# Clearing the semaphores during the last store, with SyncE waiting for that store in GpSimd's place

## Chip, cores and metric

One core of one Trainium2 chip. The metric is the device time of one execution in microseconds (us); the kernel before has a median of 121.06 us over three runs (121.06 to 121.23). Engines are called PE (TensorE), DVE (VectorE), ACT (ScalarE), POOL (GpSimd) and SP (SyncE), as in the profile.

## The reference

```python
x, y: (1024, 4096) float32
z = x + y
out = 0.5 * z * (1 + np.tanh(np.sqrt(2 / np.pi) * (z + 0.044715 * z ** 3)))
```

An addition followed by the tanh form of GELU, elementwise: 33.55 MB are read and 16.78 MB are written.

## The kernel before

Each input is seen as 128 partitions of 32,768 numbers. SP's queue issues four loads of 8,192 columns of x and four of y in turn (`load_x`, `load_y`), then three stores of 16,384, 10,240 and 6,144 columns (`store`, L130 to L132). The arithmetic runs in sixteen chunks of 2,048 columns: POOL adds y into the z tile (DVE does it for chunk 0; L145), ACT squares into PSUM (L150), DVE forms the polynomial (L156), ACT applies the sigmoid (L161) and DVE multiplies back into z (L168). The order on each engine is written out by hand in four lists, one for each queue (SP, POOL, ACT, DVE), and issued from these in the `while any(queues)` loop (L209). None of this is touched by the change.

After the last list is empty, `tc.close()` (lines shown as L223 in the profile) adds the end of the program. It is a block of instructions of its own, behind the block with the work: SP waits for every DMA and for the other engines, two barriers over all five engines follow, and POOL clears the eleven semaphores 99 to 109, which the program counted with, so that the next execution starts from zero. A barrier here is: SP, ACT, PE and DVE each add one to semaphore 96 with a DRAIN, POOL waits until that is four, takes it back, adds four to semaphore 97, and each of the others waits for that and takes one off.

`wait_late` (L26 to L58), called last in the kernel (L225), edits that end block. SP's wait for everything loses the wait for the last store, whose semaphore is 103 (it has to count 32: two DMAs with 16 each). POOL's pair, a DRAIN and an EVENT_SEMAPHORE_RANGE_CLEAR of 99 to 109, moves from between the two barriers to behind the second one, and the DRAIN gets the wait for semaphore 103. So the last instructions of the program are, in the kernel before:

```
SP    waits for all DMAs but the last store, for DVE and POOL
all   barrier 1
all   barrier 2
POOL  DRAIN, waits for semaphore 103 >= 32
POOL  EVENT_SEMAPHORE_RANGE_CLEAR 99 to 109
```

`begin_early` (L11 to L23) moves the first two loads ahead of the barrier at the start; the change doesn't touch it.

Of the kernel before, what the change touches and what calls it, by code (L numbers as in the profile page):

```python
# [25 lines left out]
def wait_late(nc):  # L26


    body, end = nc.main_func.blocks[1:3]
    SP, POOL = mybir.EngineType.SP, mybir.EngineType.Pool  # L30
    last = [i for i in body.instructions if isinstance(i, mybir.InstDMACopy)][-1]
    (sem,) = [u.id for u in last.sync_info.on_update]
    all_done = end.instructions[0]
    clear = next(i for i in end.instructions if isinstance(i, mybir.InstDrain) and i.is_reset_sema)
    assert all_done.engine == SP and clear.engine == POOL and clear.sync_info is None
    waits = all_done.sync_info.on_wait
    its = [w for w in waits if w.id == sem]
    assert len(its) == 1
    rest = [w for w in waits if w.id != sem]

    def drain(old, waits, **reset):
        return mybir.InstDrain(
            name=old.name, engine=old.engine, debug=old.debug,
            sync_info=mybir.SyncInfo(on_wait=waits, on_update=[]), **reset
        )

    at = end.instructions.index(clear)
    clears = [
        drain(
            clear, its, is_reset_sema=True,  # L50
            reset_range_start=clear.reset_range_start, reset_range_stop=clear.reset_range_stop,
        ),
        end.instructions[at + 1],
    ]
    assert isinstance(clears[1], mybir.InstISA) and clears[1].engine == POOL
    del end.instructions[at : at + 2]
    end.instructions[0] = drain(all_done, rest, is_reset_sema=False)
    end.instructions.extend(clears)  # L58


@with_exitstack
def kernel(
# [160 lines left out]
    tc.compile()  # L223
    begin_early(nc, 2)
    wait_late(nc)  # L225


# [28 lines left out]
```

## Time and profile before

| what | value |
|---|---|
| median of three runs | 121.06 us (121.06 to 121.23) |
| the profiled execution, its own time | 121.08 us |
| its span, first to last instruction of the program | 118.9 us (118.914 in the trace) |
| outside the span, of the time | 2.17 us |
| DVE busy | 73.7 us, 62% |
| POOL busy | 69.7 us, 59% |
| ACT busy | 61.0 us, 51% |
| DMA queue | 98.6% of 16 engines' span, 50.33 MB |
| last store (3,072 KB), issue to landing | 11.9 us |

Times in the profile count from the span's start. An instruction that belongs to an engine's sequencer (waits, barriers, DRAIN, the clearing of semaphores, DMA issues) is shown with a q behind the engine's name and isn't counted as busy. A view of one source line lists, for each engine and operation, how many there were, their shortest, median and longest time in ns, and the first and last start in us. The table of stretches gives for each stretch its length, each engine's busy time, and the share of the DMA engines' time that was used. The trace also holds the moment of every change of a semaphore, that of the runtime's semaphores too, after the span's end.

### The profile page before, as it was taken

Reading aid. Unit: us, or ns where it says so; the run is one execution under the profiler, and the core shown is the slowest. Engines: PE = TensorE matmul, PEld = TensorE weight load, DVE = VectorE, ACT = ScalarE, POOL = GpSimd, SP = SyncE. Lnnn points to the kernel's source line nnn. Section 1 sums busy time; section 2 is a strip of 40 time slices with the busy share of each in tenths; the row PEclk is TensorE's granted clock in tenths of the full one; section 3 lists DMA queues with packets and bytes.
Section 4 is the critical chain, followed back from the end, with each engine's and each line's share of the span. In section 5 each row is a group of like instructions: output and inputs, shape, how many; then the busy total and the mean of one; then the engine's idle time right before and its main releaser. Section 6 shows DMA issues by size and latency. Waiting matters only on the chain.

```text
span 118.9 us, 170 instructions
## 1 busy us (share of the span) xinstructions
DVE 73.7 (62%) x35; ACT 61.0 (51%) x34; POOL 69.7 (59%) x19
## 2 busy tenths in 40 slices
DVE  0000000635799995749999958999994999990000
ACT  4000000064888865197698657888829769800000
POOL 0000000699995199999959999959999990000000
DMA  7989898989999898989899998998898889999996
GB/s 254 452 364 518 353 529 353 518 364 474 408 430 452 364 518 353 529 353 518 364 474 408 408 474 353 529 529 353 353 683 375 353 353 441 441 441 441 397 397 265
DMA packets 1584, 50.33 MB, mean 423 GB/s; under 512 B 176, under 2 KB 176, under 8 KB 176
## 3 DMA queue, kind: packets, MB, share of 16 engines
q1 hardware_dynamic: 1584, 50.33, 98.6%
HBM read 33.55 MB, written 16.78 MB: 423 GB/s over the span
## 4 chain that ended last, share of the span: by engine, by line
DMA 51%; POOL 26%; POOLq 4%; DVE 4%; DVEq 2%; ACT 2%; issue 0%; SPq 0%
DMA y<-in_y_dram 51%; POOL z L145 26%; POOLq L223 4%; DVE w L156 2%; DVEq L223 2%; DVE z L168 2%; ACT w L150 2%; SPq L121 0%; POOLq L145 0%
## 5 line engine op out<-in xcount | busy, mean ns | idle before, releaser
L145 POOL TENSOR_TENSOR z<-z,y 128x2048 f32<-128x2048 f32 x15 | 69.4, 4661 | 28.2 <-DMA y<-in_y_dram 28.2
L150 ACT ACTIVATE w<-z 128x2048 f32<-128x2048 f32 x16 | 30.1, 1882 | 37.6 <-DVE z L145 21.4
L156 DVE SCALAR_TENSOR_TENSOR w<-w,z 128x2048 f32<-128x2048 f32 x16 | 36.7, 2295 | 11.2 <-ACT w L150 11.0
L168 DVE TENSOR_TENSOR z<-w,z 128x2048 f32<-128x2048 f32 (+1 forms) x17 | 35.9, 2155 | 0.0
L161 ACT ACTIVATE w<-w 128x2048 f32<-128x2048 f32 x16 | 29.7, 1855 | 4.4 <-DVE w L156 4.3
L145 DVE TENSOR_TENSOR z<-z,y 128x2048 f32<-128x2048 f32 x1 | 2.3, 2292 | 20.4 <-DMA y<-in_y_dram 20.4
L208 ACT ACT_TABLE_LOAD x1 | 1.3, 1283 | 1.3 <-PEq L240 1.3
L207 DVE MEMSET one<- 128x1 f32 x1 | 0.1, 59 | 1.3 <-PEq L240 1.3
L240 POOL MEMSET const-float32-0.0<- 128x1 f32 x1 | 0.1, 99 | 0.2 <-issue 0.2
L208 ACT ACTIVATE one<-one 128x1 f32<-128x1 f32 x1 | 0.2, 203 | 0.0
L240 POOL MEMSET const-bfloat16-1.0<- 128x1 bf16 x1 | 0.1, 101 | 0.0
L240 POOL MEMSET const-uint8-127<- 128x1 uint8 x1 | 0.1, 101 | 0.0
L240 POOL MEMSET const-float32-1.0<- 128x1 f32 x1 | 0.1, 98 | 0.0
## 6 DMA issues: line engine op xcount, KB each, us to landing
z<-in_x_dram SPq DMA_DIRECT2D x4, 4096.0 KB, 31.3
y<-in_y_dram SPq DMA_DIRECT2D x4, 4096.0 KB, 22.2
out_dram<-z SPq DMA_DIRECT2D x1, 5120.0 KB, 15.8
out_dram<-z SPq DMA_DIRECT2D x1, 3072.0 KB, 11.9
out_dram<-z SPq DMA_DIRECT2D x1, 22.0
```

Source lines behind the costliest of these rows:

```text
L145: eng.tensor_add(out=zt[:, a:b], in0=zt[:, a:b], in1=yt[s][:, o : o + b - a])
L150: nc.scalar.activation(out=wt[c], in_=zt[:, a:b], func=act.Square, scale=root)
L156: nc.vector.scalar_tensor_tensor(out=wt[c], in0=wt[c], scalar=c1, in1=zt[:, a:b], op0=alu.add, op1=alu.mult)
L161: nc.scalar.activation(out=wt[c], in_=wt[c], func=act.Sigmoid)
L168: ins = nc.vector.tensor_mul(out=zt[:, a + o : a + o + n], in0=wt[c][:, o : o + n], in1=zt[:, a + o : a + o + n],)
L207: nc.vector.memset(one, 0.0)
L208: nc.scalar.activation(out=one, in_=one, func=act.Sigmoid)
L223: tc.compile()
L240: nc = _bacc.Bacc("TRN2", target_bir_lowering=False, num_devices=1)
```

## The change

Only `wait_late` changes. POOL's DRAIN and its clearing stay where `tc.close()` put them, between barrier 1 and barrier 2, and no longer wait for anything. The one clearing of 99 to 109 becomes two, 99 to 102 and 104 to 109, which leave out semaphore 103. At the very end SP gets one new instruction, an EVENT_SEMAPHORE that waits until 103 has counted 32 and takes 32 off. The end of the program becomes:

```
SP    waits for all DMAs but the last store, for DVE and POOL
all   barrier 1
POOL  DRAIN
POOL  EVENT_SEMAPHORE_RANGE_CLEAR 99 to 102
POOL  EVENT_SEMAPHORE_RANGE_CLEAR 104 to 109
all   barrier 2
SP    EVENT_SEMAPHORE, waits for semaphore 103 >= 32, subtracts 32
```

```diff
-    at = end.instructions.index(clear)
-    clears = [
-        drain(
-            clear, its, is_reset_sema=True,
-            reset_range_start=clear.reset_range_start, reset_range_stop=clear.reset_range_stop,
-        ),
-        end.instructions[at + 1],
-    ]
...
-    del end.instructions[at : at + 2]
-    end.instructions[0] = drain(all_done, rest, is_reset_sema=False)
-    end.instructions.extend(clears)
...
+    parts = []
+    for f, e in ((first, sem), (sem + 1, stop)):
+        if f < e:
+            nc.gpsimd.sem_clear(range(f, e))
+            parts.append(nc.cur_bb.bb.instructions.pop())
+    end[at + 1 : at + 2] = parts
+    end.append(
+        mybir.InstEventSemaphore(
+            name=clear.name, engine=mybir.EngineType.SP, debug=clear.debug,
+            sync_info=mybir.SyncInfo(
+                on_wait=[its],
+                on_update=[
+                    mybir.SyncUpdate(
+                        sync_type="semaphore", id=sem, ant_name=its.ant_name,
+                        update_mode="sem-sub-imm", update_value=its.wait_value,
+                    )
+                ],
+            ),
         )
+    )
```

SP's first wait of the end block keeps the same set of waits as before. The instructions of PE, ACT and DVE are the same, and so are all of POOL's and SP's up to the end block.

## Prediction

> **What bounds the kernel now.** I read the page first, then the table of stretches for the end, then the view of the line of the closing code (L223), then SP's waits.
>
> ```profile
> span 118.9 us, 170 instructions
> ...
> q1 hardware_dynamic: 1584, 50.33, 98.6%
> ...
> DMA y<-in_y_dram 51%; POOL z L145 26%; POOLq L223 4%; DVE w L156 2%; DVEq L223 2%; DVE z L168 2%; ACT w L150 2%; SPq L121 0%; POOLq L145 0%
> ...
> out_dram<-z SPq DMA_DIRECT2D x1, 3072.0 KB, 11.9
> ```
>
> The one DMA queue is full for 98.6% of the span: the kernel is bound by its 50.33 MB. The chain of waits names the loads and POOL's adds, but it stops at 106.7 us, where the last multiply (L168) releases the last store; the 12.2 us behind that are the store and the end of the program. They are read from stretches:
>
> ```profile
> core 0: us, DVE busy (x) ACT busy (x) POOL busy (x), PEclk, DMA share, GB/s
> ...
> 107.00:112.50 5.50, 0.00 (x0) 0.00 (x0) 0.00 (x0) 1.00 0.91 390
> 112.50:118.26 5.76, 0.00 (x0) 0.00 (x0) 0.00 (x0) 1.00 0.93 401
> 118.26:118.70 0.44, 0.00 (x0) 0.00 (x0) 0.00 (x0) 1.00 0.00 0
> 118.70:118.92 0.22, 0.00 (x0) 0.00 (x0) 0.00 (x0) 1.00 0.00 0
> ```
>
> No engine computes after 107; data moves until 118.26. Then 0.44 us pass in which nothing moves and the store's last counts arrive on semaphore 103 (the trace has the sixteenth at 118.689), and 0.22 us that are POOL's alone:
>
> ```profile
> L223 POOLq EVENT_SEMAPHORE  x2: 17/17/17, 112.0 to 112.1; - x2
> L223 SPq EVENT_SEMAPHORE  x1: 17/17/17, 112.2 to 112.2; - x1
> L223 ACTq EVENT_SEMAPHORE  x1: 17/17/17, 112.2 to 112.2; - x1
> L223 DVEq EVENT_SEMAPHORE  x1: 21/21/21, 112.2 to 112.2; - x1
> L223 PEldq EVENT_SEMAPHORE  x1: 51/51/51, 112.2 to 112.2; - x1
> L223 POOLq DRAIN  x1: 77/77/77, 118.7 to 118.7; - x1
> L223 POOLq EVENT_SEMAPHORE_RANGE_CLEAR  x1: 95/95/95, 118.8 to 118.8; - x1
> ```
>
> Barrier 2 is over at 112.2, so four engines leave the program 6.5 us before POOL, whose DRAIN (118.713 to 118.790) and clearing (118.819 to 118.914) end the span. SP's waits show the other wait of the end block, for the middle store:
>
> ```profile
> SPq L223 <- DMA out_dram<-z: 4.2, 1, 4.2
> ```
>
> It ends at 111.4 and is left as it is.
>
> The time doesn't end with the span: 121.08 - 118.914 = 2.17 us lie around it. The trace's record of semaphore changes shows what follows. Semaphore 2, which the program never uses, is changed nine times in each of four groups, two ahead of the span and two that end behind it:
>
> ```
> last ahead of the span  -0.375 -0.341 -0.302 -0.258 -0.235 -0.124 -0.086 -0.052 -0.005
> first at the end       112.454 112.488 119.441 119.484 119.507 119.605 119.645 119.679 119.726
> second at the end      120.514 120.548 120.587 120.630 120.653 120.751 120.789 120.823 120.870
> ```
>
> I read each group as a token that goes up through five engines and back down. At the end two engines have passed it on at 112.49 and the third at 119.441, so the third is POOL. SP's first instruction stands at 0.000, when the changes at -0.052 and -0.005 are only just made, and other engines start 0.18 to 0.32 us after theirs: SP is the turning point, the fifth (-0.235). I take the order PE, ACT, POOL, DVE, SP. Between the two groups at the end, semaphores 3 to 255 are changed in blocks of 51, from 119.625 to 120.290. The last change, 120.870, lies 1.956 us behind the span, which is nearly all of the 2.17. I therefore count the time to that point, with 0.21 us for what is left; the trace doesn't say where the clock of the metric stands, and rival C is the case in which it stops sooner.
>
> **What the Trainium skill says.** "Runtime: NRT & Kernel Launch", section "The ~15µs preamble/postamble breakdown", describes a barrier that is passed on across the five engines, about 44 ns a hop, then a reset of 51 semaphores for each engine and a second barrier. The trace agrees in kind (hops of 23 to 111 ns, blocks of 51); its own times are used, since the page's 1.5 us for each of the first two stages is more than stands here (1.956 us for everything). "Perfetto Trace Analysis", section "Sequencer-only Instruction (DRAIN, etc)", says that a sequencer's record holds the execution alone, and that neither the wait nor the spreading of a semaphore change is in it: POOL's DRAIN agrees, 77 ns long after a wait of over 6 us, 24 ns behind the last count. "DMA Instruction — HWDGE (DVE, Sync)" on that page says that a DMA's count is written only after its data is confirmed, and can be late when that goes to HBM: 118.254 for the last data and 118.689 for the last count here. The change can't touch these 0.44 us.
>
> **Part by part.**
>
> *POOL's DRAIN and clearing move ahead of barrier 2.* What moves is one DRAIN (77 ns) and one clearing (95 ns), no DMA; they pass barrier 2's POOL instructions on POOL's own queue. From 118.713 to 118.914, 0.201 us leave the path. They now begin at about 112.15, and barrier 2 waits for them.
>
> *One clearing becomes two.* Another 95 ns by the same row. With DRAIN, two clearings and gaps of 29 ns: 77 + 2 x 95 + 2 x 29 = 0.33 us later for barrier 2, so PE leaves at about 112.8 rather than 112.45, POOL at some 113.1 with the 0.53 us that it needs below. The cover is the store, until 118.689: 5.6 us are left. Without that cover it would cost 0.33. Whether clearing during a running DMA slows it isn't shown; no clearing touches 103, and I take nothing, with +-0.05 us.
>
> *SP's new wait.* It ends with the last count. Rows for it: in barrier 2 SP's record starts 17 ns after the count is there and lasts 17 ns, its subtraction visible at the end. So 118.689 + 0.017 + 0.024 = 118.73, allowing POOL's slower 24 ns once; the span ends there, 0.18 us sooner. Nothing of the program is queued behind it on SP; behind it stands SP's turn in the runtime's barrier, for which all wait.
>
> *The way from the program to the barrier.* This is the largest term. POOL takes 119.441 - 118.914 = 0.527 us from its last instruction to its turn. That now lies under the store and is replaced by SP's way out, which the trace doesn't show: SP left 7 us before its turn came. PE, which is first and waits for nobody, changed semaphore 97 at 112.232 and took its turn at 112.454: 0.222 us. From below SP's way is bounded by two instructions at its own 55 to 68 ns in the end block, 0.11 us, from above by POOL's 0.53 as the slowest one seen. I take PE's 0.222, since SP steps faster than PE but may have more to do. Then SP's turn is at 118.73 + 0.222 = 118.95 instead of 119.507: 0.555 us sooner (0.67 to 0.25 at the ends).
>
> *The way back.* In the kernel before DVE has to pass the token on twice in 121 ns, and its second change is 98 ns after SP's. Now it did its first long ago, and I expect a hop like the others (34 to 47 ns): 0.06 us more. From PE's 119.726 on, everything (PE's block of resets to 120.290, then 0.22 us to the next turn, then the second token) follows PE's turn and moves as a whole.
>
> Sum: 0.555 + 0.06 = 0.61 us. Against the profiled execution, 121.08 - 0.61 = 120.47 us; it lies 0.02 above the median, so the median would be 120.45. Three runs lay 0.17 apart, so I round to 120.5. The path after the change is the store's last count, SP, and the barrier; POOL is late nowhere.
>
> **Rivals.** A measurement of this kernel can tell about 0.2%, 0.24 us, from no change.
>
> A, the forecast: SP's way out is short, 0.11 to 0.35 us, gain 0.48 to 0.73: 120.35 to 120.6. For it: PE's 0.222, and the barrier at the end within the 2.17 us.
>
> B: SP's way out is as long as POOL's. Then only the 0.18 us of the program, the two hops above POOL's place (119.441 to 119.507, 0.066) and DVE's 0.06 are won: 0.31 us, 120.77. For it: POOL's 0.527 is the only way out seen right after a wait for a DMA. Against it: POOL steps slower after its DRAIN.
>
> C: no more than the program's end counts, or the gain is in the scatter. If the metric stops with the span, 0.18 us are won, 120.9, within what can't be told. For it: the clock's place isn't shown. Against it: the semaphore changes behind the span fit the 2.17 us so well.
>
> D, slower: what SP does between the program and its turn was hidden for 7 us, as its turn came after POOL's. If it holds a load from memory, it lands on the path in full. The same section of the Runtime page has about 1.3 us for such a load at the start; estimated with it, SP's turn is at 118.73 + 0.222 + 1.3 = 120.25, 0.74 later than 119.507, less 0.06: 121.76. It decides from a way out of 0.84 us (0.777 to SP's old turn, and 0.06). Against it: PE's and ACT's ways out (ACT at most 0.3) have no room for one; for it, SP owns the only DMA queue used.
>
> **How the numbers follow.** A 0.52, B 0.15, C 0.21, D 0.12. The prediction is A's, 120.5. Faster by over 0.2% are A and nearly all of B: 0.66, within 0.2% C and a little of B: 0.22, slower 0.12. The range has to reach B and C, and at the low end A's best 120.35 less some scatter: 120.3 to 121.05; it leaves out D and the tails.
>
> **What would show it.** The span should end at 118.7 to 118.75, with SP's EVENT_SEMAPHORE as its last row, and POOL's DRAIN and two clearings at 112.1 to 112.5. On semaphore 2 the first four changes should come before 113.5 and the fifth at about 118.95, DVE's next within 50 ns. A fifth change at 119.25 is B; one after 119.5 is D and makes the prediction wrong. If it comes at 118.95 and the time is still 120.9, C is right. A last count on 103 that isn't at 118.6 to 118.8 would be a change of the store that I don't expect.

## The result and the profile after

| | before | after |
|---|---|---|
| median of six runs each | 121.09 us (121.03 to 121.23) | 120.38 us (120.37 to 120.97) |
| ratio, with its 95% interval | | 0.995 (0.9931 to 0.9969) |
| profiled execution | 121.08 us | 120.49 us |
| its span | 118.914 us | 118.830 us |
| last count of the store on semaphore 103 | 118.689 | 118.796 |
| last change of semaphore 2, first group | 119.726 | 119.135 |
| last change of semaphore 2, second group | 120.870 | 120.280 |

The kernel became 0.71 us faster by the medians, 0.59 by the two profiled executions. The span is only 0.08 us shorter: six sevenths of the gain in the profiled executions lie behind the last instruction that the profile shows. From the page of the kernel after:

```profile
span 118.8 us, 172 instructions
...
q1 hardware_dynamic: 1584, 50.33, 98.7%
...
out_dram<-z SPq DMA_DIRECT2D x1, 3072.0 KB, 11.9
```

The store itself is as before: 11.9 us from issue to landing, and the DMA queue as full. Two instructions more are there, the second clearing and SP's new wait. The table of stretches, cut at this execution's own last data and last count:

```profile
107.00:112.50 5.50, 0.00 (x0) 0.00 (x0) 0.00 (x0) 1.00 0.92 395
112.50:118.34 5.84, 0.00 (x0) 0.00 (x0) 0.00 (x0) 1.00 0.91 391
118.34:118.80 0.46, 0.00 (x0) 0.00 (x0) 0.00 (x0) 1.00 0.00 0
118.80:118.84 0.04, 0.00 (x0) 0.00 (x0) 0.00 (x0) 1.00 0.00 0
```

Behind the last count 0.04 us are left of the span, where there were 0.22. This execution issued its last store 0.09 us later than the one of before and had its last count 0.11 later; that is why 0.08 of span, and not 0.19, show. Counting from the last count takes this out. The closing code's line in the kernel after (L231 is before's L223), from 112 us on, and then the line of the clearing:

```profile
L231 POOLq DRAIN  x2: 34/58/83, 112.0 to 112.2; - x2
...
L231 SPq EVENT_SEMAPHORE  x2: 17/17/17, 112.4 to 118.8; - x2
```

```profile
L50 POOLq EVENT_SEMAPHORE_RANGE_CLEAR  x2: 53/60/66, 112.1 to 112.1; - x2
```

POOL's DRAIN and both clearings are over by 112.3, and one row of 17 ns on SP, at 118.8, is what stands behind the store. (The DRAIN of 34 ns is barrier 2's own.) SP's waits (who waited for whom, total us, times, longest) have it as their first row here. It puts the releaser down to SP itself, where the trace has the DMA's last count 17 ns ahead of that row's start; the second row is the wait for the middle store, as before:

```profile
SPq L231 <- SPq L231: 6.4, 1, 6.4
SPq L231 <- DMA out_dram<-z: 4.2, 1, 4.2
```

The token of the runtime's barrier, read from the trace's record of semaphore 2:

```
before  112.454 112.488 119.441 119.484 119.507 119.605 119.645 119.679 119.726
after   112.736 112.770 112.975 113.019 118.971 119.015 119.053 119.087 119.135
```

Four changes, not two, now lie under the store, and the fifth, SP's, comes 0.175 us behind the last count. In both kernels the second group ends 1.145 us behind the first, and the time is 0.21 us more than the moment of its last change: 120.870 + 0.21 = 121.08 and 120.280 + 0.21 = 120.49. The other executions, whose times and spans are on record, agree: the time less the span is 2.18 us on average in 32 of the kernel before and 1.68 us in the six of the kernel after.

### The profile page after: what moved, and what is told of

Read it like the earlier page. It is cut to its first block, busy times and chain, and to the rows that moved or that the text cites. A ratio compares the mean times of both kernels' runs of the same rounds, so it can differ in the third digit from the quotient of the medians.

```text
span 118.8 us, 172 instructions
## 1 busy us (share of the span) xinstructions
DVE 73.7 (62%) x35; ACT 61.0 (51%) x34; POOL 69.7 (59%) x19
## 4 chain that ended last, share of the span: by engine, by line
DMA 51%; POOL 26%; POOLq 4%; DVE 4%; DVEq 2%; ACT 2%; issue 0%; SPq 0%
DMA y<-in_y_dram 51%; POOL z L153 26%; POOLq L231 4%; DVE w L164 2%; DVEq L231 2%; DVE z L176 2%; ACT w L158 2%; SPq L129 0%; POOLq L153 0%
## 6 DMA issues: line engine op xcount, KB each, us to landing
out_dram<-z SPq DMA_DIRECT2D x1, 3072.0 KB, 11.9
```

## Experiments

The theory is that a different engine is late, and that each engine has its own way from the program to its turn in the runtime's barrier and its own place in it: POOL third and slow, SP last and quick. The first rival is that the clearing behind the store was what cost. A second is that any engine but POOL would do as well. The measure is the distance from the store's last count to the last change of the barrier's first group, taken from each profiled execution; before has 1.037 us, after 0.339. Each kernel's edit is against the kernel after.

### POOL waits, with the clearing early

```diff
-            name=clear.name, engine=mybir.EngineType.SP, debug=clear.debug,
+            name=clear.name, engine=mybir.EngineType.Pool, debug=clear.debug,
```

> The clearing stays early, as in the changed kernel, but POOL and not SP makes the last wait and the subtraction. Theory (the engine that is last out of the program decides: POOL needs 0.53 to 0.55 us to its turn in the runtime's barrier and stands before DVE and SP in it): POOL's turn comes 0.04 + 0.55 = 0.59 us behind the last count of the store, the barrier's last change 0.88 behind it (1.04 in the kernel before, 0.34 in the changed one), and the time is 0.16 us under the kernel before, about 120.92. Rival (the clearing behind the store is what cost, itself and by making POOL slow to leave): POOL's turn comes some 0.25 us behind the last count, the time is 0.5 us under the kernel before, about 120.6.

Measured: 120.97 us, ratio to before 0.9988 (0.9976 to 0.9999). The last row of its program, from the view of the closing line behind 118 us:

```profile
L231 POOLq EVENT_SEMAPHORE  x1: 17/17/17, 118.7 to 118.7; - x1
```

POOL's row ends at 118.761, its turn comes at 119.323: the way out takes 0.562 us, although nothing was cleared there and no DRAIN stands ahead of it. The barrier's last change is 0.888 us behind the last count; 0.88 was expected. So taking the clearing away from behind the store wins 0.15 us, and the rest of the gain belongs to POOL being the one that is late. The rival's 120.6 falls.

### SP waits and clears everything behind the store

```diff
-    for f, e in ((first, sem), (sem + 1, stop)):
-        if f < e:
-            nc.gpsimd.sem_clear(range(f, e))
-            parts.append(nc.cur_bb.bb.instructions.pop())
-    end[at + 1 : at + 2] = parts
+    nc.sync.sem_clear(range(first, stop))
+    parts.append(nc.cur_bb.bb.instructions.pop())
+    del end[at : at + 2]
     end.append(
-        mybir.InstEventSemaphore(
+        mybir.InstDrain(
+            name=reset.name, engine=mybir.EngineType.SP, debug=reset.debug, is_reset_sema=True,
+            reset_range_start=first, reset_range_stop=stop,
+            sync_info=mybir.SyncInfo(on_wait=[its], on_update=[]),
...
+    end.extend(parts)
```

> SP makes the last wait, and the whole clearing of 99 to 109 stays behind the store, on SP. Theory (the engine decides): the clearing costs its own duration, 0.05 to 0.15 us with its gap; SP's turn 0.27 us behind the last count instead of 0.175, the barrier's last change 0.46 behind it; about 120.5, some 0.6 under the kernel before. Rival (the clearing behind the store is what cost): most of the gain is gone, the time within 0.25 us of the kernel before, about 120.9.

Measured: 120.45 us, ratio 0.9948 (0.9935 to 0.9961). The two rows behind the store in its profile:

```profile
L48 SPq EVENT_SEMAPHORE_RANGE_CLEAR  x1: 51/51/51, 118.9 to 118.9; - x1
```

```profile
L223 SPq DRAIN  x1: 7/7/7, 118.9 to 118.9; - x1
```

The whole clearing stays where it was in time, and the barrier's last change is 0.401 us behind the last count, 0.06 more than in the changed kernel, where 0.12 more was expected. DRAIN, gap and clearing end 0.125 us behind the last count, where the bare wait ends 0.034 us behind it; but SP's way out is then 0.111 us instead of 0.140. Moving the wait to SP gives nearly all of the gain without moving the clearing ahead. This is the mirror of the run before, and the two together show the cause: the engine, not the clearing. Why POOL needs so long to its turn, no run here shows.

### PE, ACT or DVE waits

The same one-word edit with `PE`, `Activation` and `DVE`, to see whether the place in the barrier counts.

> As the changed kernel, but PE makes the last wait and the subtraction. Theory (the token of the runtime's barrier starts at PE, goes up by ACT, POOL and DVE to SP and back): PE's turn 0.06 + 0.22 us behind the last count, then four hops up (0.14) and four down (0.22, DVE's 0.1 turn with them): last change 0.64 us behind the last count, 0.3 more than with SP; about 120.68. Rival (the order in the barrier doesn't matter, any engine but POOL will do): 120.4 to 120.45.

> As the changed kernel, but ACT makes the last wait and the subtraction. Theory of the order: ACT is second in the barrier, so PE's turn comes early at 112.7 and ACT's at the end; with a way out of 0.15 to 0.3 us its turn is 0.2 to 0.34 us behind the last count, three hops up (0.11) and four down (0.22): last change 0.53 to 0.67 behind the last count; 120.57 to 120.71. Rival (the order doesn't matter): 120.4 to 120.45.

> As the changed kernel, but DVE makes the last wait and the subtraction. Theory of the order (DVE is fourth, next to the turning point): with a way out of 0.15 to 0.25 us its turn is 0.19 to 0.29 us behind the last count, then SP's 0.02, DVE's second 0.10 and three hops of 0.12: the last change 0.43 to 0.53 behind the last count, between SP's 0.34 and ACT's 0.50 or just above; 120.47 to 120.57. Rival (the way out alone decides): the same as SP within 0.05 us.

The last row of PE's and of DVE's kernel behind 118 us:

```profile
L231 PEldq EVENT_SEMAPHORE  x1: 51/51/51, 118.8 to 118.8; - x1
```

```profile
L231 DVEq EVENT_SEMAPHORE  x1: 21/21/21, 118.9 to 118.9; - x1
```

The first group on semaphore 2 in each profiled execution, with the last count of its store ahead of it:

```
POOL  118.720   112.702 112.736 119.323 119.366 119.389 119.488 119.527 119.561 119.608
PE    118.790   119.148 119.183 119.221 119.265 119.288 119.387 119.426 119.460 119.507
ACT   118.699   112.708 118.877 118.915 118.959 118.982 119.079 119.119 119.154 119.200
DVE   118.831   112.674 112.709 112.914 119.062 119.085 119.183 119.223 119.257 119.304
```

All five engines side by side. The way out runs from the end of the waiting row to that engine's turn. The time behind the last count is how far the span ends behind that count in the profile, plus the time less the span, averaged over all executions of the kernel (5 to 32):

| who waits | place | way out, us | barrier's last change behind the last count, us | time behind the last count, us | median, us | ratio to before, interval |
|---|---|---|---|---|---|---|
| POOL, clearing last (before) | 3 | 0.527 | 1.037 | 2.40 | 121.09 | |
| POOL | 3 | 0.562 | 0.888 | 2.24 | 120.97 | 0.9988 (0.9976 to 0.9999) |
| PE | 1 | 0.279 | 0.717 | 2.08 | 120.82 | 0.9979 (0.9972 to 0.9987) |
| ACT | 2 | 0.140 | 0.501 | 1.70 | 120.58 | 0.996 (0.9948 to 0.9973) |
| DVE | 4 | 0.183 | 0.473 | 1.81 | 120.64 | 0.9959 (0.9947 to 0.9972) |
| SP (after, run again below) | 5 | 0.140 | 0.339 | 1.69 | 120.46 | 0.9942 (0.9928 to 0.9955) |

The place is shown directly. With PE waiting, the first change of the group comes at 119.148 and none before; with ACT one lies early (112.708) and the second comes late; with DVE three lie early; with SP four. ACT leaves as fast as SP, yet its barrier ends 0.16 us later: its three hops up to SP (118.877 to 118.982) and DVE's longer turn are 0.16, the difference of place alone. PE was 0.08 us slower by the distance than expected, 0.06 of it in its way out and 0.02 in its row (by the median 0.14, 120.82 against 120.68). DVE's distance was as expected, its median 0.07 us above the expected range.

The times bear this out for POOL, PE, DVE and SP: for them the time behind the last count is the distance plus 1.36 us, within 0.03 (1.145 between the two groups, and 0.21 to 0.225 behind the second). For ACT it isn't: 1.86 us would follow, and it is 1.70, as with SP. In its profile the time even ends 0.09 us ahead of the second group's last change, and one hop of that group took 155 ns. It is no odd execution, for the time less the span is 1.60 to 1.69 us in all nine. So the price of ACT's place stands in the barrier but not in the time, and why stays open. That its median met the expectation is luck: its spans were longer (median 118.9 us, the changed kernel's 118.7 and 118.8), so its last counts came later. By the intervals of the medians, POOL and PE are slower than SP; ACT and DVE can't be told from it so, but DVE's 1.81 us behind the last count are 0.12 more than SP's.

### The changed kernel again

> The changed kernel itself, beside the others on one chip. 120.38 us again, within 0.1; the last change of the first group 0.34 us behind the last count. If the gain were chance of few runs, it would come back nearer to 121.

Measured: 120.46 us (120.25 to 120.52), and again 0.339 us. The gain is no accident of few runs.

### More clearings under the store

The prediction named the store as the cover of the moved clearings, and put the effect of clearing on a running DMA at nothing. These kernels add clearings of 99 to 102, which are at zero by then, behind the two of the changed kernel:

```diff
+    for _ in range(60):
+        nc.gpsimd.sem_clear(range(first, sem))
+        parts.append(nc.cur_bb.bb.instructions.pop())
     end[at + 1 : at + 2] = parts
```

> As the changed kernel, with sixty more clearings of 99 to 102 on POOL between the barriers. Theory (they are covered by the store): sixty at the 79 ns that lie between the two clearings' starts are 4.7 us; POOL's and DVE's turns move from 113.0 to 117.7, still ahead of SP's at 118.97, and the time stays at 120.4. Rival (clearing while a DMA runs slows the DMA, or the barrier behind it matters): the store's last count comes later than 118.6 to 118.85, and the time rises above 120.6.

> As before with 120 more clearings, 9.5 us. Theory: the cover is 5.95 us (DVE's turn at 113.02 to SP's at 118.97), so some 3.6 us show: PE's turn at 122.2, the last change of the first group at about 122.7, the time about 124.0; the last count on 103 as ever, 118.6 to 118.85. Rival (clearings cost less when nothing waits for them, or are hidden by more than this): under 122.

Measured: 120.79 us with sixty, ratio 0.9972 (0.9958 to 0.9986), and 123.73 us with 120, ratio 1.0219 (1.0205 to 1.0233). The added clearings in the two profiles, sixty first:

```profile
L53 POOLq EVENT_SEMAPHORE_RANGE_CLEAR  x60: 47/47/47, 112.4 to 117.1; - x60
```

```profile
L53 POOLq EVENT_SEMAPHORE_RANGE_CLEAR  x120: 47/47/52, 112.4 to 121.5; - x120
```

With 120 they end behind the store, PE's turn comes at 122.030 and the first group ends at 122.555, where 122.7 was expected: the cover has about the size that was worked out, and what lies beyond it shows. The clearings start 76 ns apart on average, where 79 was reckoned. With sixty, DVE's turn is at 117.908, well ahead of SP's 119.348, and the distance from the last count is 0.338 as ever. In the order of the barrier nothing is exposed. Yet the kernel is 0.33 us over the changed one: the last count comes at 119.174, not at 118.6 to 118.85 (with 120 at 119.356). The expectation of 120.4 was wrong. In this execution 0.16 us of it lie ahead of the store, which was issued that much later than in the second run of the changed kernel, before any added instruction ran. The other 0.19 us lie in the store: from the end of its issue to the last count it took 11.78 us, and 11.60 and 11.59 in the two runs of the changed kernel. The page of the kernel with sixty also has a line, the second here, that the changed kernel's page hasn't:

```profile
q1 hardware_dynamic: 1584, 50.33, 98.4%
q14 instruction: 1, 0.01, 0.0%
```

It is a transfer of 8 KB of instructions, 309 ns long, at 118.44. The trace's packets show a second thing: one chain of the store's packets, each starting as the one ahead ends, takes 0.96 to 1.015 us a packet from 111.75 on, where nearly all others take 0.91. Three more kernels, and this one again, were to tell these apart. The first has sixty DRAINs on POOL in place of the clearings:

```diff
+    for k in range(60):
+        parts.append(
+            mybir.InstDrain(
+                name=f"I-{5000 + k}", engine=mybir.EngineType.Pool, debug=reset.debug, is_reset_sema=False,
+                sync_info=mybir.SyncInfo(on_wait=[], on_update=[]),
+            )
+        )
     end[at + 1 : at + 2] = parts
```

> As the kernel with sixty more clearings, but with sixty DRAINs on POOL in their place: as many instructions in the same place, and no semaphore is written. If writing semaphores during the store is what made that kernel 0.33 us slower than the changed one, this one stands at 120.4 to 120.5. If it is the number of instructions (a longer program), or anything else that they share, it stands near 120.8.

> The kernel with sixty more clearings again, on the chip and in the call of the DRAINs. If its 120.79 us is its own, it comes back within 0.15; if it was the chip or the hour, it stands at 120.4 to 120.5.

> Thirty more clearings in place of sixty. The traces of the three kernels with 60 or 120 more instructions hold one transfer of 8 KB of instructions (309 ns) in the last 1 us of the store, which the changed kernel's trace doesn't. If that transfer is what cost, thirty fit ahead of it: no such transfer, the last count at 118.7 to 118.85, the time 120.35 to 120.5. If each clearing slows the store, half of the 0.33 to 0.4 us shows: 120.55 to 120.65, without the transfer.

The last puts the sixty clearings on SP, ahead of barrier 2:

```diff
     end[at + 1 : at + 2] = parts
+    for _ in range(60):
+        nc.sync.sem_clear(range(first, sem))
+        end.insert(at + 1, nc.cur_bb.bb.instructions.pop())
```

> The sixty more clearings on SP, whose program is less than half as long as POOL's (30 instructions before they are added, POOL's 69), between the barriers. If the 8 KB transfer of instructions slows the store and SP's program needs none: no such transfer in the trace, last count 118.65 to 118.85, time 120.35 to 120.5. If writing semaphores sixty times slows the store: no transfer, and still 120.75 to 120.9. If the transfer is there again, the two stay apart undecided; then 120.55 or more.

| added under the store | median, us | ratio to before, interval | issue's end to last data, us | last data to last count, us | the slow chain, us a packet | 8 KB of instructions at |
|---|---|---|---|---|---|---|
| nothing (changed kernel) | 120.38 | 0.995 (0.9931 to 0.9969) | 11.14 | 0.46 | one packet of 1.00 | none |
| nothing (again) | 120.46 | 0.9942 (0.9928 to 0.9955) | 11.24 | 0.35 | one packet of 1.00 | none |
| 60 DRAINs on POOL, to 116.4 | 120.60 | 0.9948 (0.9932 to 0.9964) | 11.26 | 0.48 | 0.93 to 0.98, seven packets to 117.6 | 117.98 |
| 30 clearings on POOL, to 114.5 | 120.59 | 0.9951 (0.9932 to 0.9971) | 11.55 | 0.48 | 1.00 to 1.02, three packets to 115.0 | 118.10 |
| 60 clearings on POOL, to 117.1 | 120.79 | 0.9972 (0.9958 to 0.9986) | 11.26 | 0.51 | 0.96 to 1.015, to 117.7 | 118.44 |
| 60 clearings on POOL (again) | 120.84 | 0.9965 (0.9953 to 0.9977) | 11.44 | 0.49 | 0.96 to 1.01, to 117.8 | 118.26 |
| 120 clearings on POOL, to 121.5 | 123.73 | 1.0219 (1.0205 to 1.0233) | 11.51 | 0.52 | 0.96 to 1.02, to 118.8 | 118.32 |
| 60 clearings on SP, to 116.2 | 121.05 | 0.9997 (0.999 to 1.0004) | 11.49 | 0.77 | 0.96 to 1.06, to 116.8 | 118.68 |

The DRAINs' 120.60 lies between the two cases of their expectation, thirty clearings had the time of the second case but with the transfer, and with SP the transfer is there too, so the question as it was put stays undecided. (The counts of 30 and 69 instructions for SP and POOL stand in no trace; the changed kernel's has 28 and 38.)

By the times, sixty clearings delay the kernel: by some 0.3 us on POOL (in the run beside the changed kernel's second the two intervals lie apart, and the repeat came within 0.05 us of that run), and by 0.6 us on SP, which is all of the change's gain. The 0.1 to 0.2 us of the DRAINs and of the thirty clearings are not shown, as their intervals overlap with the changed kernel's. Nor is the length of one store a firm measure: in the kernel in which DVE waits, with nothing added, the store took 11.82 us from the end of its issue to the last count, in the seven others with nothing added 11.56 to 11.60.

By the packets, the slow chain lasts about as long as the added instructions do (to 115.0 for clearings until 114.5, to 117.8 for clearings until 117.1); DRAINs lengthen its packets by some 0.03 us and clearings by some 0.09. Its data is the last of the store to end in all six kernels with more instructions. On POOL the transfer stands behind another chain, which ended its data earlier. These are the two chains with thirty clearings, as start and length of each packet:

```
slow   112.017 1.020  113.033 1.001  114.022 1.006  115.024 0.926  115.946 0.912  116.855 0.912  117.763 0.926
other  111.747 0.912  112.656 0.912  113.564 0.912  114.472 0.912  115.380 0.912  116.289 0.912  117.197 0.912  118.105 0.309 (instructions)
```

So where the last data is late on POOL, the slow chain makes it late, and not the transfer. With SP the transfer starts at 118.68, right behind the slow chain, whose last data ends at 118.69. The last count then comes 0.77 us behind the data, where the other traces have 0.35 to 0.52. That the transfer, 316 ns long here, held it up fits, but one execution doesn't show it. What makes the chain slow stays open: semaphores written by clearings can't be all of it, since the DRAINs lengthen its packets too, and as every execution here was taken with the profiler, none tells whether the recording of the added instructions has a part. The changed kernel has no such transfer, and its two clearings leave one packet of 1.00 us, where before has one of 0.98.

## Why the prediction was right

**The bound and the place of the gain.** Right. The data ends as before, and the gain is in what stands between the store's last count and the runtime's second barrier. The measured 1.037 - 0.339 = 0.698 us against the sum's 0.61, and 0.71 by the medians.

**POOL's DRAIN and clearing leave the path.** Predicted 0.18 us for the program's end; measured 0.225 us behind the last count before and 0.034 after, 0.19. The experiment in which POOL only waits finds 0.149, since POOL's way out after a bare wait is 0.035 longer.

**One clearing becomes two, under the store.** Predicted 0.33 us later for barrier 2, covered. PE's turn moved from 112.454 to 112.736, but 0.085 us of that were there ahead of barrier 1 (the last of SP's waits for the work is over at 111.707 instead of 111.622), so 0.20 us are the change's own. The two clearings took 53 and 66 ns in place of 95, and POOL used to wait for PE's DRAIN at this place, which now lies under the clearings. All of it is covered, as SP's turn comes at 118.971. That clearing slows no DMA holds for the two clearings as far as the times can tell; with sixty the end came 0.3 to 0.6 us later.

**SP's new wait.** Predicted 17 ns behind the count and 24 ns long; measured 17 and 17.

**The way out.** This term was mis-sized. PE's 0.222 us was taken for SP's; measured are 0.140 us in both runs of the changed kernel. The lower bound of 0.11, two steps of SP's own, was nearer than the engine chosen as a likeness, and PE itself took 0.279 when it was made to wait. (From the end of its row, as the others are measured here, PE's 0.222 is 0.235.) Nothing in the trace of before tied SP to PE; that the guess came within 0.08 us is luck in part. Measured from the last count, the term brings SP's turn 0.08 us ahead of the forecast and is nearly the whole difference between 0.61 and 0.70. As a gain it is 0.527 - 0.140 = 0.39 us, over half of all.

**Two hops fewer, and DVE's turn.** 0.066 us as predicted, as DVE's and SP's first changes no longer wait for POOL's. DVE's next change follows SP's by 44 ns instead of 98; 0.054 against 0.06. The four terms, 0.19 + 0.39 + 0.066 + 0.054, make up the 0.70.

**Rivals.** B falls with SP's 0.140. C falls: both profiled executions end 0.21 us behind the second group and differ by 0.59 in both, and with POOL waiting the program ends at 118.761, ahead of the changed kernel's 118.830, yet the time is 0.48 us longer. So the metric reaches beyond the program's end. That it ends just behind the second barrier fits 13 of the 14 profiled executions, and not the one in which ACT waits. D falls too: nothing slow stands on SP's way. Not tried is a cut of the 0.46 us between the last data and the last count, which no edit here touched.

**A reading to limit.** The prediction took a sequencer's record to hold no wait, which fits POOL's DRAIN. It doesn't fit every row: one of SP's in the kernel before lasts 4.236 us, from 107.219 to 111.455, and holds the wait for the middle store, whose last count is at 111.432.

```profile
L223 SPq EVENT_SEMAPHORE  x6: 17/28/4236, 107.2 to 112.2; - x6
```

## What to carry to other kernels

The program doesn't end with its last instruction: ask which engine is the last to leave, how long it takes to its turn in the runtime's barrier, and where it stands there; here the same wait on SP instead of POOL was worth 0.55 us, with not one instruction fewer. Let the engine wait last that turns the barrier round and leaves quickly (SP here), and put everything that needn't wait under the last store. Keep that cover short, though: sixty clearings that no engine waited for, under the store, still delayed the end by 0.3 us on POOL and 0.6 us on SP.

## What the runs showed that was not expected

- After a bare wait POOL's way out of the program takes 0.56 us, PE's 0.28, DVE's 0.18, ACT's and SP's 0.14; behind a clearing it is 0.03 us shorter, for POOL (0.527) as for SP (0.111).
- ACT, made to wait, ends the barrier 0.16 us later than SP, and the time doesn't show it.
- A clearing of semaphores takes 47 to 67 ns on POOL for four or six of them, 95 ns for eleven behind the long wait; on SP 32 to 43 ns for four and 51 ns for eleven, behind a long wait too.
- In all six kernels with thirty or more added instructions a transfer of 8 KB of instructions stands near the end of the store. With thirty clearings POOL's turn comes 0.69 us behind ACT's; with sixty, as in the changed kernel, 0.205.
- While clearings run, one chain of the store's packets takes some 1.00 us a packet where 0.91 is usual.
